# Side work beside a feed-forward stage: stepped by the time of the products, the modulation rows fetched whole through GpSimd's queue

## The chip, the cores and the metric

One core of one Trainium2 chip runs the whole program once. The metric is the device time of that run in microseconds (us), lower being better. The core's engines are TensorE (PE; its weight loads are listed as PEld), VectorE (DVE), ScalarE (ACT), GpSimd (POOL) and SyncE (SP, which here only issues transfers).

## The reference

Two transformer blocks follow each other on 512 tokens of 1024 features, all in fp32. What this case turns on is the first block's feed-forward layer, and two things of the second block that depend on its weights and on `c_2`, not on the tokens:

```python
# end of block 1 (FF1): D_FF = 2816
x = x + (silu(h2 @ w_gate) * (h2 @ w_up)) @ w_down
# block 2: the modulation, six vectors of 1024 = 48 rows of 128
c_act = silu(c)
mod = (c_act @ w_mod + b_mod)
sh1, sc1, g1, sh2, sc2, g2 = split(mod, 6)
h = rms(x, norm1_w) * (1 + sc1) + sh1
...
y_ssm = s5(u, lam_re, lam_im, log_dt, b_re, b_im, ...)   # powers of a complex diagonal, from weights alone
x = x + g1 * (mixed @ w_out)
h2 = rms(x, norm2_w) * (1 + sc2) + sh2
x = x + g2 * conv_ffn(h2, w_up, conv_w, conv_b, w_down)   # FF2
```

The rows 0 to 39 of `mod` hold the five vectors sh1 to sc2; the last eight, 40 to 47, hold g2, which nothing reads before the second feed-forward layer's last additions.

## The kernel before, in words

An fp32 weight block is loaded into a tile `raw` (512 KB, two buffers, issued by SP), split by ACT into `whi` (L365) and by DVE or POOL into the remainder `wlo` (L367); activations are split in the same way into a hi and a lo half (`hl`, `hd`). A product of 128 features by 512 tokens is three matmuls per slice of 128 inputs (hi by hi, lo by hi, hi by lo; all at L259), which sum into one PSUM bank.

FF1 (`ffn`, with `w3` and `w4`) walks over 22 hidden tiles in chunks of 2, 4, 4, 4, 4 and 4. A hidden tile is a gate product and an up product of 24 matmuls each. DVE reads the two banks (`fg`, L1299, and `fu`, L1302), multiplies them (L1303) and makes the lo half of the result `hd` (L494); ACT makes the silu and the hi half. A chunk is followed by the eight down products of the chunk before, each added to a tile of `x` by DVE (L1323). The three `acc` banks are handed round: the fourth product after one may not start until DVE has read that one's bank.

Beside FF1 run two "fillers", generators that `fill()` advances by one step each, once after a hidden tile and once after a down product. `modulation()` makes the 48 rows of `mod`: each row's weights, 128 by 1024, come as two halves of 128x512 (256 KB) through SP's queue into `wm` (three buffers, L1060), and one DVE instruction multiplies a half by silu(c) and sums it (L1061, followed by a short read of the accumulator). `s5_tables()` makes the tables of the S5 scan in four quads: POOL multiplies and adds tiles (`bb`, `bs`, `s5e`, `s5g`; small doubling steps `s5r` and `s5t` at L1077 to L1082, six rounds on 8 to 256 columns), PE transposes `s5e` (L1178) and makes a product of `s5g`; POOL, ACT and SP write the results to DRAM. `LAG` steps lie between parts of one quad.

The engines work in order, each through its own list. Which instruction stands where in a list is decided by a scheduler at build time, from its own estimates; an instruction whose input isn't there holds up all that is behind it on its engine.

FF2 is the second call of `ffn` (`w8`, `w9`); it has seven PSUM banks instead of three and no fillers.

Of the kernel before, what the change touches and what calls it, by code (L numbers as in the profile page):

```python
# [12 lines left out]
ALU = mybir.AluOpType  # L13
# [37 lines left out]
LAG = 4  # L51
# [12 lines left out]
# ------------------------------------------------------------------ layout  # L64
# [29 lines left out]
def w_plan():  # L94
    """name -> list of (input, row0, n_k, columns): one contiguous [128, n_k * n] block each."""
    plan = {}
    plan["w1"] = [("w_in", 0, 8, c) for _, c in W1_CHUNKS]
    plan["w2"] = [("w_out", 0, 8, c) for c in _c256(D)]
    plan["w3"] = [(w, 0, 8, c) for c in _c256(DFF) for w in ("w_gate", "w_up")]
    plan["w4"] = [("w_down", r * P, n, c) for r, n in FCH for c in _c256(D)]  # L100
    plan["w5"] = [("w_in_2", 0, 8, c) for _, c in W5_CHUNKS]
    plan["w6"] = [("w_glu_2", 0, 4, c) for c in _c256(512)]
    plan["w7"] = [("w_out_2", r, 4, c) for r in (0, 512) for c in _c256(D)]
    plan["w8"] = [("w_up_2", 0, 8, c + o) for c in _c256(DFF) for o in (0, DFF)]
    plan["w9"] = [("w_down_2", r * P, n, c) for r, n in FCH for c in _c256(D)]
    return plan
# [18 lines left out]
def pvec(i):  # L125
    """per-partition vectors, name -> [128, n]"""
# [36 lines left out]
def consts():  # L163
    """constants of the shapes alone, name -> [128, n]"""
    f = np.float32
    o = {}
    p = np.arange(P)[:, None]
    o["ident"] = np.eye(P, dtype=f)
    o["onesD"] = np.full((P, P), 1.0 / D, f)
    o["ones512"] = np.full((P, P), 1.0 / 512, f)  # L170
    y = np.arange(512)[None]
    dist = p + 384 - y
    o["dist"] = np.where(dist >= 0, dist, BIG).astype(f)
    mult = ((dist <= 128) * 1 + (dist % 4 == 0) * 1 + (dist % 16 == 0) * 1) * (dist >= 0)
    o["nlm"] = np.where(mult > 0, -np.log(np.maximum(mult, 1)), BIG).astype(f)
    n = np.arange(32)[None, None]
    t = (np.arange(NT)[None, :, None] * P + p[:, :, None])
    dc = t - (16 * n + 31)
    o["distc"] = np.where((dc >= 0) & (n < 31), dc, BIG).astype(f).reshape(P, NT * 32)
    o["rsum"] = (p % 32 == np.arange(32)[None]).astype(f)  # L180
    o["bd"] = ((p // HD) == (np.arange(P)[None] // HD)).astype(f) / HD
    o["sgn"] = np.where(p < 64, -1.0, 1.0).astype(f)
    return o
# [46 lines left out]
# ------------------------------------------------------------------ kernel  # L230
def build(tc, I, out, PV, PVN, CS, CSN, CS1, CSN1):
# [11 lines left out]
    def copy(cat, n, dst, src, scale=None):  # L243
        """on the scalar engine or on the vector engine"""
# [39 lines left out]
    # ---- constants and per-partition vectors  # L284
# [18 lines left out]
    def tables(after=None, name="natural_log_exp_and_others"):  # L303
        """activation tables that the next functions share"""
        if after is None:
            nc.scalar.preload_act_table_set(name)
        else:
            with tc.issue_after(after.ins if hasattr(after, "ins") else after):
                nc.scalar.preload_act_table_set(name)
# [3 lines left out]
    # ---- weights: load, split into two 12-bit parts whose sum is the weight  # L313
# [10 lines left out]
    def cut(name, j):  # L324
        """block j as pieces: (first k, last k, first column, last column) each, with its source"""
# [11 lines left out]
    class _Lazy:  # L337
# [3 lines left out]
        def get(self):  # L341
            """the hi and lo parts; the pieces that come next are on their way too"""
# [29 lines left out]
    def hold_after(piece):  # L372
        """no piece beyond this one is prepared ahead of need"""
        limit[0] = queue.index(piece) + 1

    def go_on(*after):
        """pieces are prepared ahead again, behind the instructions given"""
# [65 lines left out]
    def proj_f(ps, w, x, m, k0=0, cs=ALL):  # L443
        """ps[m-feature, token] = W[:, m].T @ x"""
# [4 lines left out]
    def proj_group(group, x, order, cs=ALL):  # L449
        """several (ps, w, m) at once, the contraction outermost"""  # L450
# [6 lines left out]
    def proj_late(ws, x, early, late, done):  # L457
        """all 8 feature tiles; the first three wait for the late part of x last"""
# [13 lines left out]
    def proj_t(ps, w, x, t, n, o=0):  # L472
        """ps[token, o:o + n] = x[:, token].T @ W"""
# [13 lines left out]
    def split_scaled(dst, src, scale_col):  # L487
        """dst hi/lo of src * scale_col"""
# [7 lines left out]
    def rsqrt_(o, ms, scale=1.0):  # L496
        """o = (ms * scale + eps) ** -0.5, from the tables"""
# [3 lines left out]
    def rsqrt_m2(pool, tag, r, ms):  # L501
        """r = -2 * (ms + eps) ** -0.5, with a Newton step"""
# [6 lines left out]
    def head_norm(pool, wide, dsts, src, nh):  # L509
        """dsts[i][tok, heads, dup, 64] = -128 * src[tok, heads, 64] / rms, the heads in order"""  # L510
# [19 lines left out]
    # gains with the factors that the norms leave open: -1/128 per head norm, -1/2 per feature norm  # L530
# [12 lines left out]
    # ================================================================ block 1  # L543
# [6 lines left out]
    # ---- x, its squares, the unscaled normed input; the first products run along as the tiles of x come in  # L550
# [50 lines left out]
    # ---- bias tables of the causal attentions  # L601
# [11 lines left out]
    # compress chain inputs  # L613
# [11 lines left out]
    # ---- keys, values and gates of the sparse attention; queries and keys of all heads  # L625
# [15 lines left out]
    def kv_p(n):  # L641
        """two query tiles at a time"""
# [28 lines left out]
    def turn2(src):  # L671
        """both query tiles of a pair of heads side by side"""
# [6 lines left out]
    def kv_x(n):  # L679
        """hi and lo of the keys, the same on both halves of the partitions"""  # L680
# [12 lines left out]
    def qa_x(t):  # L693
        """the hi part of the queries on the lower half of the partitions, the lo part on the upper half"""
# [31 lines left out]
    # ---- compressed keys and values  # L726
# [65 lines left out]
    # ---- compressed branch, all tiles at once  # L792
# [28 lines left out]
    # ---- group norm of a finished feature tile, split for the next product  # L821
# [20 lines left out]
    # ---- softmax of one query tile, 4 heads  # L842
# [58 lines left out]
    # ---- stick-breaking: what is left of the stick before a key is the product of 1 - sigmoid over the later keys  # L901
# [32 lines left out]
    # ---- dilated  # L934
# [24 lines left out]
    # ---- short convolution  # L959
# [43 lines left out]
    def tok_norm(pool, parts, r, w="onesD", cs=ALL):  # L1003
        """-2 / rms of every token, on all partitions; the parts add up to the squares"""
# [26 lines left out]
    # ---------------------------------------------------------------- feed-forward 1, with work of block 2 beside it  # L1031
# [18 lines left out]

    def modulation():
# [3 lines left out]
        mh = s5p.tile([P, 2, 48], F32, name="mh")  # L1055
        yield
        for j in range(48):
            for n in range(2):
                wm = s5p.tile([P, 512], F32, tag="wm", bufs=3, name="wm")
                nc.sync.dma_start(wm, I["wmod"][j][:, n * 512:(n + 1) * 512])  # L1060
                V.tensor_tensor_reduce(wm, wm, cb[:, n * 512:(n + 1) * 512], 1.0, 0.0, ALU.mult, ALU.add, mh[:, n, j:j + 1])  # L1061
            yield
        V.tensor_tensor(modT, mh[:, 0], mh[:, 1], op=ALU.add)
        V.tensor_tensor(modT, modT, V1("b_mod"), op=ALU.add)
        dbg("mod", modT)
        yield

    def s5_tables():
# [3 lines left out]
        def cmul(o_r, o_i, a_r, a_i, b_r, b_i, shape, E):  # L1072
            """o = a * b, complex; o may not overlap a or b"""
# [41 lines left out]
        # (a - 1) / lambda  # L1115
# [17 lines left out]
        # mag ** 8 and the rotations of 8, 16, .. 256 steps  # L1133
# [14 lines left out]
        for q in range(4):  # L1148
# [16 lines left out]
            # input to the state at the end of a chunk of 8 tokens  # L1165
# [17 lines left out]
            # state to output, powers 0..8  # L1183
# [11 lines left out]
            # within a chunk  # L1195
# [15 lines left out]
            # rotations of 0..63 chunks  # L1211
# [11 lines left out]
    fillers = [s5_tables(), modulation()]  # L1223

    def fill():
        for f in fillers:
            next(f, None)

    def ffn(wn_up, wn_down, hin, hidden, add_down, after=lambda: None, start=None, tail=None, banks=(acc,)):
# [4 lines left out]
        def up(c):  # L1234
            r, n = FCH[c]
            for j in range(r // 2, (r + n) // 2):
                ws = weights(wn_up, 2 * j), weights(wn_up, 2 * j + 1)
                for m in range(2):
                    ps = []
                    for a in range(2):  # L1240
# [4 lines left out]
                        ps.append(p_)  # L1245
                    hid[2 * j + m] = hidden(2 * j + m, *ps)
                    after()

        def down(c):
            r, n = FCH[c]  # L1250
            last = c == len(FCH) - 1
            for k in range(8 if not (last and tail) else 8 - TAIL):
# [3 lines left out]
                after()  # L1256
# [9 lines left out]
    def norm_tail(pool, tot, r, after, hold, before=None, TAIL=TAIL, NPOS=NPOS):  # L1266
        """the last feature tiles by halves of the tokens: the norm of one half runs beside the products of the other"""
# [42 lines left out]
    def sum_squares(tot, k, src, cs, sq):  # L1310
        """adds to tot, except for the last one, which is returned"""
# [21 lines left out]
    def modulated(n, r, dst, cs, tmp):  # L1333
        """hi/lo of x * r * norm_w * (1 + sc) + sh"""
# [13 lines left out]
    def start_u(cs):  # L1348
        if cs is HALVES[0]:
            for f in fillers:  # L1350
                for _ in f:
# [15 lines left out]
    # ================================================================ block 2  # L1367
# [48 lines left out]
    # ---- S5: chunks of 8 tokens; partitions hold (place, channel) or the state  # L1416
# [21 lines left out]
    def crossed(dst, src, t, sign):  # L1438
        """the imaginary part times t into the real rows, and minus the real part times t into the imaginary rows"""
# [55 lines left out]
    # ---- k, v, q  # L1495
    tokn = {}

    def kv_p(n):
        """two query tiles at a time"""
# [34 lines left out]
    # ---- sliding-window attention  # L1534
# [4 lines left out]
    def keep(k, src, cs, tot, first, gain, n, scale=1.0):  # L1539
        """the hi/lo of a finished feature tile times its gain, and its squares; the norm is applied after the product"""  # L1540
# [13 lines left out]
    def swa_s(n):  # L1554
        """softmax of query tile i, the 4 heads of one key/value head"""
# [57 lines left out]
    # ---- gated linear unit, and its share of the output projection  # L1613
# [71 lines left out]
    # ---------------------------------------------------------------- feed-forward 2  # L1685
# [26 lines left out]
    ffn("w8", "w9", h2, hidden2, down2, start=started, banks=(tr, sc, acc) if B2 else (acc,))  # L1712
# [28 lines left out]
```

## Time and profile before

| what | value |
|---|---|
| runs | 1321.51, 1324.22 and 1327.34 us, median 1324.22 us |
| profiled execution, first to last instruction (span) | 1323.2 us |
| PE busy | 1247.0 us, 94% of the span |
| DVE busy | 864.9 us, 65% |
| ACT, POOL busy | 501.5 us, 38%; 386.4 us, 29% |
| mean granted clock of TensorE | 0.964 of full |

The profile has no other time of its own execution than the span; it lies between the lowest and the median run. Busy shares are means over stages with different limits: FF1 runs from 319 us to some 718 us, the attention part of block 2 follows, FF2 begins at about 970 us. A waiting time counts only where the engine that waits is the one that the rest waits for.

### The profile page before, as it was taken

The page shows a single profiled execution, that of the slowest core. Times are in us where ns is not written, and L with a number is a line of the kernel's source. Part 1 is how long each engine was busy: PE and PEld are TensorE (multiplying, and loading weights), DVE is VectorE, ACT ScalarE, POOL GpSimd, SP SyncE. Part 2 cuts the span into 40 slices and gives each one's busy share as a digit, 9 for nine tenths or more (in the row PEclk, how much of TensorE's full clock was granted, in tenths as well). Part 3 has the DMA queues.
Part 4 walks back from the last instruction along what each step waited for, and adds up shares of the span by engine and source line. Part 5 has one row for each costly group of instructions (what it writes and reads, how often), then busy time and mean ns, then how long its engine had stood idle before and what let it go on. Part 6 is the DMA issues. An engine that isn't in the chain of part 4 may idle for free.

```text
span 1323.2 us, 17207 instructions
## 1 busy us (share of the span) xinstructions
PE 1247.0 (94%) x6269; PEld 1005.0 (76%) x6269; DVE 864.9 (65%) x1615; ACT 501.5 (38%) x862; POOL 386.4 (29%) x403
## 2 busy tenths in 40 slices
PE   7999999999979878999999989979899999999998
PEld 6888765667857657788888978757888888888887
DVE  7668768767988878745445778795855443435362
ACT  5334466445213122322233432663454333333330
POOL 3000004012327439092511143025152423232300
PEclk8999999999999999999999986779899999999999
DMA  5431111126567676643434763331132423232321
GB/s 213 140 123 49 50 32 49 51 77 197 160 198 252 196 248 200 187 147 111 145 109 156 268 175 116 80 96 58 39 99 84 135 85 107 82 108 82 105 87 63
DMA packets 163668, 164.11 MB, mean 124 GB/s; under 512 B 12160, under 2 KB 127760, under 8 KB 163584
## 3 DMA queue, kind: packets, MB, share of 16 engines
q1 hardware_dynamic: 154240, 146.43, 36.2%
q0 software_dynamic: 4256, 12.29, 3.0%
q10 hardware_dynamic: 5088, 4.29, 1.0%
q8 instruction: 49, 0.80, 0.3%
q14 instruction: 35, 0.29, 0.1%
HBM read 149.39 MB, written 15.43 MB: 125 GB/s over the span
## 4 chain that ended last, share of the span: by engine, by line
PE 53%; DVE 16%; DMA 8%; issue 4%; ACT 2%; POOL 0%; DVEq 0%; SPq 0%; ACTq 0%; POOLq 0%
PE acc L259 31%; PE sc L259 10%; PE tr L259 9%; DMA wm<-in_wmod_dram 6%; DVE wm L1061 3%; DMA raw<-in_w_dram 2%; DVE wlo L367 2%; PE po L259 1%; ACT whi L365 1%; DVE hd L494 1%; DVE z L1441 1%; DVE x L1655 1%; DVE z L1442 1%; PE tr L1591 0%; DVE sqsum L1317 0%
## 5 line engine op out<-in xcount | busy, mean ns | idle before, releaser
L259 PE MATMUL acc<-hl,whi 128*128 128x512 f32 (+1 forms) x1624 | 489.5, 385 | 20.9 <-DVE fg L1299 7.5
L259 PEld LDWEIGHTS acc<-hl,whi 128*128 128x128 f32 x1624 | 298.8, 192 | 90.3 <-issue 19.1
L365 ACT ACTIVATE whi<-raw 128x1024 fp32r<-128x1024 f32 (+1 forms) x187 | 193.9, 1039 | 378.4 <-PE acc L259 178.0
L259 PE MATMUL acc<-hl,wlo 128*128 128x512 f32 (+1 forms) x812 | 311.2, 383 | 0.0
L367 DVE TENSOR_TENSOR wlo<-raw,whi 128x1024 fp32r<-128x1024 f32 (+1 forms) x133 | 170.3, 1282 | 67.4 <-ACT whi L365 64.7
L367 POOL TENSOR_TENSOR wlo<-raw,whi 128x1024 fp32r<-128x1024 f32 x54 | 132.2, 2450 | 265.9 <-ACT whi L365 265.9
L259 PEld LDWEIGHTS acc<-hl,wlo 128*128 128x128 f32 x812 | 155.1, 191 | 32.3 <-issue 2.4
L259 PE MATMUL acc<-hd,whi 128*128 128x512 f32 (+1 forms) x472 | 146.4, 393 | 19.3 <-DVE fu L1302 9.2
L259 PEld LDWEIGHTS acc<-hd,whi 128*128 128x128 f32 x472 | 87.9, 191 | 42.7 <-issue 12.7
L259 PE MATMUL acc<-whi,hl 128*128 128x256 f32 (+1 forms) x544 | 111.2, 295 | 1.6 <-ACT tok L246 1.6
L1061 DVE CUSTOM_DVE_ANT_0 wm<-wm,cb 128x512 f32<-128x512 f32 x96 | 87.1, 929 | 30.3 <-DMA wm<-in_wmod_dram 29.3
L259 PEld LDWEIGHTS acc<-whi,hl 128*128 128x128 f32 x544 | 91.1, 199 | 6.2 <-ACT tok L246 3.0
L259 PE MATMUL acc<-hd,wlo 128*128 128x512 f32 (+1 forms) x236 | 92.5, 392 | 0.0
L259 PE MATMUL acc<-wlo,hl 128*128 128x256 f32 (+1 forms) x272 | 79.9, 294 | 0.5 <-DVE wlo L367 0.5
L259 PE MATMUL tr<-hl,whi 128*128 128x512 f32 (+1 forms) x240 | 72.8, 386 | 0.0
L259 PE MATMUL sc<-hl,whi 128*128 128x512 f32 x208 | 64.9, 393 | 0.0
L914 POOL TENSOR_SCALAR_AFFINE_SELECT keep<-keep 128x128 f32<-128x128 f32 x16 | 9.3, 595 | 185.2 <-ACT keep L908 184.4
L259 PEld LDWEIGHTS acc<-wlo,hl 128*128 128x128 f32 x272 | 54.3, 200 | 2.6 <-DVE wlo L367 1.0
L259 PEld LDWEIGHTS acc<-hd,wlo 128*128 128x128 f32 x236 | 45.3, 192 | 9.5
L259 PEld LDWEIGHTS tr<-hl,whi 128*128 128x128 f32 x240 | 44.5, 188 | 9.8
L1323 DVE TENSOR_TENSOR x<-x,acc 128x512 f32<-128x512 f32 (+1 forms) x49 | 31.9, 655 | 28.8 <-PE acc L259 28.7
L259 PE MATMUL tr<-hl,wlo 128*128 128x512 f32 (+1 forms) x120 | 46.3, 386 | 0.0
(422 smaller groups left out, 1963.8 us busy)
## 6 DMA issues: line engine op xcount, KB each, us to landing
raw<-in_w_dram SPq DMA_DIRECT2D x177, 512.0 KB, 4.3
wm<-in_wmod_dram SPq DMA_DIRECT2D x96, 256.0 KB, 3.9
xk<-in_xT_dram SPq DMA_DIRECT2D x16, 256.0 KB, 4.7
d_g<-s5g POOLq DMA_DIRECT2D x4, 576.0 KB, 4.3
gt<-d_g SPq DMA_DIRECT2D x4, 576.0 KB, 4.0
w1c<-in_w1k_dram SPq DMA_DIRECT2D x8, 256.0 KB, 5.7
w1c<-in_w1v_dram SPq DMA_DIRECT2D x8, 256.0 KB, 7.1
raw<-in_w_dram SPq DMA_DIRECT2D x8, 256.0 KB, 2.7
```

Source lines behind the costliest of these rows:

```text
L259: nc.tensor.matmul(o, lhsT=l, rhs=r, start=start, stop=stop, **k)
L365: act(hi[:, :m], raw[:, :m], AF.Copy)
L367: E.tensor_tensor(lo[:, :m], raw[:, :m], hi.bitcast(F32)[:, :m], op=ALU.subtract)
L494: V.tensor_tensor(dst[:, 1], src, dst.bitcast(F32)[:, 0], op=ALU.subtract)
L914: G.affine_select(g[:, d], g[:, d], fill=1.0, **past)
L1061: V.tensor_tensor_reduce(wm, wm, cb[:, n * 512:(n + 1) * 512], 1.0, 0.0, ALU.mult, ALU.add, mh[:, n, j:j + 1])
L1323: V.tensor_tensor(x[k][:, cs], x[k][:, cs], ps[:, cs], op=ALU.add)
L1441: V.scalar_tensor_tensor(dst[re], src[im], sign, t[im], op0=ALU.mult, op1=ALU.mult)
L1442: V.scalar_tensor_tensor(dst[im], src[re], -sign, t[re], op0=ALU.mult, op1=ALU.mult)
L1655: V.tensor_tensor(x[k][:, cs], x[k][:, cs], t[:, cs], op=ALU.add)
```

## The change

`fill` now takes the time of the product beside it: each filler has a rate, and is advanced whenever time times rate has summed up to a whole step. `ffn` calls it with 5.5 after each product of a hidden tile (twice per tile, before it was once) and with 0.7 per slice after a down product. `LAG` goes from 4 to 2. A row of the modulation is fetched whole (128x1024, 512 KB, two buffers) by a transfer that GpSimd issues, and reduced by one DVE instruction. Only rows 0 to 39 belong to FF1; rows 40 to 47 are made in FF2, one step after each product, with a second copy of silu(c).

```diff
-LAG = 4
+LAG = 2
+NWM = 2
+S5_RATE = 0.185
+MOD_RATE = 0.14
...
+    mh = cpool.tile([P, 48], F32, name="mh")
+
+    def mod_rows(pool, cb, j0, j1):
+
+        for j in range(j0, j1):
+            wm = pool.tile([P, D], F32, tag="wm", bufs=NWM, name="wm")
+            nc.gpsimd.dma_start(wm, I["wmod"][j])
+            V.tensor_tensor_reduce(wm, wm, cb, 1.0, 0.0, ALU.mult, ALU.add, mh[:, j:j + 1])
+            yield
+        V.tensor_tensor(modT[:, j0:j1], mh[:, j0:j1], V1("b_mod")[:, j0:j1], op=ALU.add)
+        yield
+
     def modulation():
         cb = s5p.tile([P, D], F32, name="cb")
         nc.sync.dma_start(cb, I["cbc"])
         act(cb, cb, AF.Silu)
-        mh = s5p.tile([P, 2, 48], F32, name="mh")
         yield
-        for j in range(48):
-            for n in range(2):
-                wm = s5p.tile([P, 512], F32, tag="wm", bufs=3, name="wm")
-                nc.sync.dma_start(wm, I["wmod"][j][:, n * 512:(n + 1) * 512])
-                V.tensor_tensor_reduce(wm, wm, cb[:, n * 512:(n + 1) * 512], 1.0, 0.0, ALU.mult, ALU.add, mh[:, n, j:j + 1])
-            yield
-        V.tensor_tensor(modT, mh[:, 0], mh[:, 1], op=ALU.add)
-        V.tensor_tensor(modT, modT, V1("b_mod"), op=ALU.add)
...
+        yield from mod_rows(s5p, cb, 0, 40)
...
-    fillers = [s5_tables(), modulation()]
-
-    def fill():
+    fillers = [[s5_tables(), S5_RATE, 0.0], [modulation(), MOD_RATE, 0.0]]
+
+    def fill(us):
+
         for f in fillers:
-            next(f, None)
...
+            f[2] += us * f[1]
+            while f[2] >= 1.0:
+                f[2] -= 1.0
+                next(f[0], None)
...
+                        if a == 0:
+                            after(5.5)
                     hid[2 * j + m] = hidden(2 * j + m, *ps)
-                    after()
+                    after(5.5)
...
-                after()
+                after(0.7 * n)
...
-    ffn("w8", "w9", h2, hidden2, down2, start=started, banks=(tr, sc, acc) if B2 else (acc,))
+    cb2 = fp.tile([P, D], F32, name="cb2")
+    nc.gpsimd.dma_start(cb2, I["cbc"])
+    act(cb2, cb2, AF.Silu)
+    late = mod_rows(fp, cb2, 40, 48)
+    ffn("w8", "w9", h2, hidden2, down2, after=lambda us: next(late, None), start=started, banks=(tr, sc, acc) if B2 else (acc,))
```

Comments were removed too, so that lines of the new kernel carry other numbers: L1082 to L1087 are the former L1077 to L1082, L370 the former L367, L497 the former L494, L1310, L1313 and L1314 the former L1299, L1302 and L1303.

The first place is POOL's list in FF1, first quad. In the rows below `wm` is a row of the modulation weights, `s5t` and `s5r` are the doubling steps, `bb`, `bs` and `s5u` parts of the second quad's input. Before, POOL's list has no rows and these steps stand alone; after, the rows 8 to 14 stand between them (8 to 11 in the first line, 12 and 13 on either side of one step, 14 at the end):

```order
L1060 DMA wm<-in_wmod_dram 128x1024 x4
L1083 TENSOR_TENSOR s5t<-s5r,ro_i 128x8
...
L1083 TENSOR_TENSOR s5t<-s5r,ro_i 128x64
L1060 DMA wm<-in_wmod_dram 128x1024
L1084 TENSOR_TENSOR s5r<-s5r,s5t 128x8x8
L1060 DMA wm<-in_wmod_dram 128x1024
L1086 TENSOR_TENSOR s5t<-s5r,ro_r 128x64
...
L1175 TENSOR_TENSOR s5e<-bb,pw_r 128x1024
L1087 TENSOR_TENSOR s5r<-s5r,s5t 128x8x32
L1060 DMA wm<-in_wmod_dram 128x1024
```

Between row 11 and row 12 stand 19 small steps, between row 13 and row 14 another 19 instructions, among them `s5e` on 1024 columns. A row can be fetched only after them.

The second place is DVE's list at the same rows. The reductions of rows 10 to 14 stand between the readings of the banks (`fg`, `fu`), the products' second halves (`wlo`) and `hd`:

```order
L1061 ISA wm,mh<-wm,cb 128x1024
L497 TENSOR_TENSOR hd<-fu,hd 128x512
L1061 ISA wm,mh<-wm,cb 128x1024
L1310 SCALAR_TENSOR_TENSOR fg<-acc,r_3100 128x512
L370 TENSOR_TENSOR wlo<-raw,whi 128x512
L1061 ISA wm,mh<-wm,cb 128x1024
L1061 ISA wm,mh<-wm,cb 128x1024
L1313 SCALAR_TENSOR_TENSOR fu<-acc,r_3100 128x512
L370 TENSOR_TENSOR wlo<-raw,whi 128x512
L1314 TENSOR_TENSOR fu<-fu,fg 128x512
L1061 ISA wm,mh<-wm,cb 128x1024
L497 TENSOR_TENSOR hd<-fu,hd 128x512
```

(the short reads of the accumulator are left out.) Behind each reduction stands the reading of a bank that PE will want again. The last of the 40 reductions stands behind the gate bank of the 13th hidden tile, at the same place as the last of the 96 did before.

The third place is POOL's list at the start of FF2. Before it is `wlo` alone, 44 of them; after, the copy of c and the rows 40 to 47 stand among the first eleven:

```order
L370 TENSOR_TENSOR wlo<-raw,whi 128x1024 x3
L1724 DMA cb_8607<-in_cbc_dram 128x1024
L370 TENSOR_TENSOR wlo<-raw,whi 128x1024
L1060 DMA wm<-in_wmod_dram 128x1024 x2
L370 TENSOR_TENSOR wlo<-raw,whi 128x1024
L1060 DMA wm<-in_wmod_dram 128x1024
L370 TENSOR_TENSOR wlo<-raw,whi 128x1024 x2
L1060 DMA wm<-in_wmod_dram 128x1024 x2
```

SP's list loses all its `wm` transfers, which before stood two to four at a time between the loads of `raw`.

## Rows read from the trace of the kernel before

**Rows 1.** Two stretches of FF1, then FF2: busy time of each engine, clock, transfers.
```profile
319.00:545.50 226.50, 199.77 (x848) 157.05 (x847) 191.11 (x403) 58.98 (x80) 107.87 (x134) 0.95 0.68 212
545.50:718.00 172.50, 171.51 (x775) 137.93 (x774) 90.72 (x104) 52.22 (x67) 64.67 (x113) 1.00 0.42 129
980.00:1320.00 340.00, 339.19 (x1467) 275.15 (x1465) 153.74 (x194) 113.79 (x142) 89.42 (x37) 1.00 0.32 94
```

**Rows 2.** The products' line alone (L259) in two stretches: PE, PEld, clock, transfers.
```profile
319.00:545.50 226.50, 197.19 (x832) 154.30 (x831) 0.95 0.68 212
340.00:360.00 20.00, 20.00 (x88) 16.24 (x87) 1.00 0.72 217
```

**Rows 3.** Waits from 319 to 545.5 us: in total, times, the longest.
```profile
DVE wm L1061 <- DMA wm<-in_wmod_dram: 29.3, 25, 3.0
PE acc L259 <- DVE fg L1299: 11.0, 4, 4.0
PE acc L259 <- DVE fu L1302: 9.7, 3, 6.9
```

**Rows 4.** DVE's groups of instructions, 319 to 545.5 us: busy, mean ns, idle before.
```profile
L1061 DVE CUSTOM_DVE_ANT_0 wm<-wm,cb 128x512 f32<-128x512 f32 x96 | 87.1, 929 | 30.3 <-DMA wm<-in_wmod_dram 29.3 <-ACT cb L1054 1.0
L367 DVE TENSOR_TENSOR wlo<-raw,whi 128x1024 fp32r<-128x1024 f32 (+1 forms) x33 | 41.4, 1255 | 2.7 <-ACT whi L365 2.7
L494 DVE TENSOR_TENSOR hd<-fu,hd 128x512 fp32r<-128x512 f32 x12 | 14.8, 1236 | 0.0
L1299 DVE SCALAR_TENSOR_TENSOR fg<-acc,r 128x512 f32<-128x512 f32 x13 | 8.9, 681 | 0.0
L1061 DVE DVE_READ_ACCUMULATOR2_ANT mh<- 128x1 f32 x96 | 7.6, 79 | 0.0
```

**Rows 5.** Timeline of DVE: start, duration, idle time before and what ended it.
```profile
391.82 2.14 DVE L1061 CUSTOM_DVE_ANT_0 wm<-wm,cb 128x512 f32<-128x512 f32 x1 [0.50 <-DMA wm<-in_wmod_dram]
...
397.51 0.68 DVE L1061 CUSTOM_DVE_ANT_0 wm<-wm,cb 128x512 f32<-128x512 f32 x1
...
969.55 4.17 DVE L1694 SCALAR_TENSOR_TENSOR cf<-acc,pv,cf 128x511 f32<-128x511 f32 x6 [6.48 <-ACT cf L1692]
```

**Rows 6.** Transfers issued from 319 to 545.5 us: count, KB each, median us to landing.
```profile
wm<-in_wmod_dram SPq DMA_DIRECT2D x96, 256.0 KB, 3.9
raw<-in_w_dram SPq DMA_DIRECT2D x29, 512.0 KB, 4.8
d_rot<-s5r POOLq DMA_DIRECT2D x2, 512.0 KB, 4.8
```

**Rows 7.** Timeline of POOL, first quad, while DVE is busy.
```profile
390.88 2.53 POOL L1189 TENSOR_TENSOR s5g<-s5bc,pw_r 128x1152 f32<-128x1152 f32 x1 [20.68 <-PE tr L1178]
...
396.72 0.58 POOL L1192 DMA_DIRECT2D d_g<-s5g  x1 [0.30 <-POOL s5g L1191]
...
405.28 0.21 POOL L1078 TENSOR_TENSOR s5t<-s5r,ro_i 128x8 f32<-128x8 f32 x1 [6.41 <-DMA d_et<-s5et]
...
409.11 0.67 POOL L1082 TENSOR_TENSOR s5r<-s5r,s5t 128x8 f32<-128x8 f32 x1
...
415.28 1.16 POOL L1078 TENSOR_TENSOR s5t<-s5r,ro_i 128x64 f32<-128x64 f32 x1
...
424.13 0.61 POOL L1078 TENSOR_TENSOR s5t<-s5r,ro_i 128x256 f32<-128x256 f32 x1
...
433.11 2.05 POOL L1170 TENSOR_TENSOR s5e<-bb,pw_r 128x1024 f32<-128x1024 f32 x1
```

**Rows 8.** Timeline of POOL, third quad, with no more rows on DVE.
```profile
568.30 0.20 POOL L1078 TENSOR_TENSOR s5t<-s5r,ro_i 128x8 f32<-128x8 f32 x1
...
574.11 0.30 POOL L1078 TENSOR_TENSOR s5t<-s5r,ro_i 128x64 f32<-128x64 f32 x1
...
580.18 0.61 POOL L1078 TENSOR_TENSOR s5t<-s5r,ro_i 128x256 f32<-128x256 f32 x1
...
589.44 0.45 POOL L1163 TENSOR_TENSOR bs<-bs,s5u 128x128 f32<-128x128 f32 x1
```

More of the change, by code (lines that the diff above doesn't have):

```diff
@@ L1054, in modulation @@
         act(cb, cb, AF.Silu)
-        mh = s5p.tile([P, 2, 48], F32, name="mh")
         yield
-        for j in range(48):
-            for n in range(2):
-                wm = s5p.tile([P, 512], F32, tag="wm", bufs=3, name="wm")
-                nc.sync.dma_start(wm, I["wmod"][j][:, n * 512:(n + 1) * 512])
-                V.tensor_tensor_reduce(wm, wm, cb[:, n * 512:(n + 1) * 512], 1.0, 0.0, ALU.mult, ALU.add, mh[:, n, j:j + 1])
-            yield
-        V.tensor_tensor(modT, mh[:, 0], mh[:, 1], op=ALU.add)
-        V.tensor_tensor(modT, modT, V1("b_mod"), op=ALU.add)
-        dbg("mod", modT)
-        yield
+        yield from mod_rows(s5p, cb, 0, 40)
     def s5_tables():
@@ L1221, in s5_tables, with ffn @@
             yield
-    fillers = [s5_tables(), modulation()]
-    def fill():
+    fillers = [[s5_tables(), S5_RATE, 0.0], [modulation(), MOD_RATE, 0.0]]
+    def fill(us):
         for f in fillers:
-            next(f, None)
-    def ffn(wn_up, wn_down, hin, hidden, add_down, after=lambda: None, start=None, tail=None, banks=(acc,)):
+            f[2] += us * f[1]
+            while f[2] >= 1.0:
+                f[2] -= 1.0
+                next(f[0], None)
+    def ffn(wn_up, wn_down, hin, hidden, add_down, after=lambda us: None, start=None, tail=None, banks=(acc,)):
         banks = itertools.cycle(banks)
@@ L1350, in start_u @@
             for f in fillers:
-                for _ in f:
+                for _ in f[0]:
                     pass
```

## The prediction

> **What bounds the kernel now.** I read the stretches first. FF1 falls into two: from 319 to 545.5 us PE is busy 199.8 of 226.5 us at a granted clock of 0.95, and after that, as in FF2, it is busy almost all the time at full clock [rows 1]. So PE is the limit everywhere around this change except in the first stretch, and only there can anything be won. At the full pace of 20.00 us for 88 matmuls, 0.2273 us each, the 832 matmuls of the products would take 189.1 us instead of 197.2 [rows 2]. The stretch thus loses 26.7 us to an idle PE and some 8 us to the clock, 35 us in all: the ceiling of any gain here.
>
> Next, why PE idles. It waits for DVE to read banks, `fg` and `fu`, never for anything nearer to the change [rows 3]. DVE in turn is busy 191.1 us of the stretch [rows 1], and of its idle 35.4 us (226.5 - 191.1) 29.3 are spent before a reduction whose weights haven't landed [rows 3]; no wait of DVE for a bank shows among its groups [rows 4]. That is the reading the rest hangs on: in this stretch DVE is the chain. Its work and its waits add up to the stretch, PE follows through three banks, and the last reduction ends it (PE is full from there). The order of the changed kernel puts its last reduction behind the same bank as before, that of the 13th hidden tile. So the new stretch is the sum of DVE's work and DVE's waits up to there.
>
> DVE's work is not all its own. `fg`, which reads PSUM and one SBUF tile, takes 681 ns; a half row's reduction, two SBUF tiles, has a mean of 929 ns, and single ones run from 0.68 to over 2 us [rows 4, 5]. The 2.14 us one at 391.82 lies under POOL's `s5g` of 390.88 to 393.41 [rows 5, 7]. `hd`, 1236 ns on tiles of the same size, is stretched too [rows 4].
>
> The Trainium skill, "SBUF — State Buffer", section "Who interferes with whom", states such a rule: a VectorE instruction with two SBUF inputs and a GpSimd instruction that reads SBUF exclude each other for a whole instruction, one with a single SBUF input isn't touched. The trace agrees, `fg` with 681 ns against `hd` with 1236 ns [rows 4].
>
> **The change, part by part, as DVE's sum.**
>
> Work taken off DVE: 96 half rows become 40 whole ones, the work of 80 halves. 87.1 us x 16/96 = 14.5 us go [rows 4]; with them 56 of 96 reads of the accumulator, 56 x 79 ns = 4.4 us [rows 4]. 191.1 - 18.9 = 172 us.
>
> Contention: POOL now has three quads' work and a part of the fourth beside the rows, where two and a part of the third lay before (107.9 us of POOL in the stretch, 64.7 us in the next [rows 1]). What the stretching costs now is (929 - 680) ns x 96 for the reductions and (1236 - 681) ns x 12 for `hd`, 24 + 7 = 31 us [rows 4, 5]. The change adds between nothing (while DVE waits, nothing is stretched, and it has fewer reductions) and half as much again, 15 us. I take 5, nearer to nothing for these two reasons.
>
> Waits at gaps: this is the dear part. A row's transfer is issued by POOL in its turn. With two buffers POOL may be two rows ahead, but whatever S5 work stands between two rows keeps the second back. A gap of G us on POOL makes DVE wait G + 0.6 (an issue by POOL, like that of `d_g`, 0.58 us [rows 7]) less what DVE has to do meanwhile: a whole row, some 1.24 us (an estimate: two undisturbed halves, 0.68 us each [rows 5], less the overlap of their ends), and what stands between the two reductions, each 0.68. POOL's times come from the same entries in two quads: the first, with DVE busy [rows 7], and the third, with no rows on DVE [rows 8].
> - First place, rows 12 and 14. The 19 steps from `s5t` on 8 columns to `s5t` on 64: from 405.28 to 416.44, less some 1.9 us for a wait and other entries, 9.3 us [rows 7]; from 568.30 to 574.41, 5.7 us [rows 8]. Between the reductions `fg` and `wlo`: 9.3 + 0.6 - 2.6 = 7, or 4. The second 19, with `s5e`: 416.44 to 435.16 less 1, 17.7 us [rows 7]; 574.41 to 589.89 less 2.1, 13.4 us [rows 8]. Between the reductions `fu`, `wlo` and the product: less 3.3, which gives 15, or 11. Together 22, or 15.
> - Second place, rows 20 and 22. Row 20 stands behind `s5g` and its sum, 390.88 to 396.42, 5.5 us [rows 7], an issue and eight small entries: some 8 us, less 4 of DVE's own: 4. Row 22 stands behind 27 steps up to `s5t` on 256 columns: 409.11 to 424.74, 15.6 us [rows 7], or 11.0 (568.30 to 580.79 less 1.5 for seven entries ahead) [rows 8]; less 2: 14, or 9. Together 18, or 13.
> - Third place, rows 33 to 38. Row 36 stands behind 20 of these 27 steps, 11.6 or 8.2 us by count, less 0.6: 11, or 7.5. Row 33 stands behind `s5g` (0 to 2), 37 and 38 a product apart (0 to 4). Together 17, or 8.
>
> The sum is 57 us on contended times, 36 on quiet ones. Since DVE stands idle in the later part of each gap, neither holds throughout; I take the middle, 46.
>
> The rhythm between gaps: nine rows stand beside the eight down products of the second chunk, where a cycle of two buffers allows one row in (4.8 + 0.6 + 1.24)/2 = 3.3 us (a 512 KB transfer takes 4.8 us, from SP's queue or from POOL's [rows 6]), 30 us for what PE does in 22 (8 x 12 x 0.2273). With DVE's other work there it is 0 to 8; I take 5. The idle time that isn't a wait for rows stays, 35.4 - 29.3 = 6.
>
> What costs nothing: SP loses 96 issues, so `raw` no longer stands behind halves that wait for buffers. But DVE waits for `whi` only 2.7 us in the stretch [rows 4], which bounds that gain; I count none. The rows move as many bytes each as before, 21 instead of 25 MB, at a transfer share of 0.68 [rows 1]. `LAG` and the rates move the transposes and tables forward; PE doesn't wait for POOL.
>
> The page "DMA: Bandwidth & Descriptors" of the Trainium skill, section "Anatomy of one DMA — SWDGE (gpsimd) path", gives by its formula some 3.2 us for 512 KB; an estimate by that would make the rhythm free, and the sum 5 us less. The traced 4.8 us is used.
>
> FF2: eight rows, 10 us of DVE, in a stage where DVE is busy 153.7 of 340 us [rows 1]. Its first reduction stands ahead of the first `cf`, which began at 969.55 after an idle 6.48 [rows 5]. The copy of c must be fetched, made silu of and be followed by a row: I estimate two transfers, 2 x 4.8 us, from 963 us, so DVE begins some 3 us late, beside seven banks that give PE 7 x 5.5 us to run on. Taken as 0; with the cover gone, +10.
>
> **Sum.** 172 + 5 + 46 + 5 + 6 = 234 us against 226.5: +7.5. 1323.2 + 7.5 is 1331; the median of the runs lies 1 us above the profiled span, so 1332 us. At the ends: 172 + 0 + 36 + 0 + 6 = 214 (-12.5, 1312) and 172 + 15 + 57 + 8 + 6 = 258 (+31.5, 1356). It balances at gap waits of 38.5 us.
>
> **The rivals.**
>
> *The other side: DVE comes late to its rows.* If at each of the seven gaps the row ahead has been lying in its buffer for some 3 us (one row and a `wlo` of 1.26 us still before DVE [rows 4]), the quiet 36 becomes 15. Then DVE needs 172 + 15 + 11 = 198, still above PE's own 189, and the kernel takes 1324 + 198 - 226.5 = 1296; with half of that lead, waits of 25, it is 1306, which I give it. From waits under 38.5 us on, the change gains. For it speaks that DVE is busy 191 of 226.5 us before [rows 1]; against it that DVE waited 25 times for rows before, with three buffers and a queue that did little else [rows 3].
>
> *No change:* the gaps run at quiet times and contention stays: 172 + 5 + 38 + 5 + 6 = 226, 1324 us. What eight rows give, the gaps take.
>
> *FF2's start not covered:* 1332 + 10 = 1342.
>
> *Rows that land late from GpSimd.* If POOL's part in starting a transfer is held up by DVE, each row lands a few us later: 40 rows by 1 us in the rhythm of two buffers give up to +20 us, 1352. Against it: `d_rot`, 512 KB from POOL's queue, landed in the same 4.8 us as `raw` from SP's [rows 6]. The Trainium skill speaks for it, "SBUF — State Buffer", section "SBUF: two separate sides": transfers that GpSimd issues are starved while VectorE copies in a two-port mode, and it advises another queue.
>
> **How the numbers follow.** About 0.5%, 6.6 us, is what a measurement of this kernel can tell from no change. Chances: the main case 0.48 (its own range 1315 to 1352; slower 0.32, within the bound 0.14, faster 0.02), DVE late 0.22 (faster 0.20, same 0.02), no change 0.18 (same 0.14, slower 0.02, faster 0.02), FF2 0.05 and late rows 0.07 (slower). Together faster 0.24, same 0.30, slower 0.46. The range goes from 1305 to 1350; above lie the worst gaps and most of the late rows, below an unhindered lead, 2 in 10 together.
>
> **What would show it.** In the changed profile, DVE's wait for `wm` should grow from 29.3 to about 50 us with single waits of 7 to 15 us, before rows 12, 14, 22 and 36, each behind a run of `s5r` and `s5t` on POOL; DVE's reductions should be 40 in FF1 and sum to under 75 us; PE's waits for `fg` and `fu` should lie right behind those waits, the stretch to the last of the 40 should take about 234 us, and PE should be full after it and in FF2. I am wrong if DVE's wait stays under 38 us, if rows land in 6 us or more, or if the stretch ends elsewhere than at the last reduction.

## The result and the profile after

The changed kernel takes 1341.58 us (median of 4 runs, 1340.69 to 1344.02) against 1322.87 us before (the three runs of the table of before and a fourth): a ratio of 1.0137, 95% interval 1.0114 to 1.0160. It is slower by 18.7 us; 8 were forecast. The profiled executions have spans of 1339.3 and 1323.2 us, 16.1 us apart.

Where the 16.1 us lie is read from four marks. FF1's last sum of squares ahead of it ends 1.6 us later than before; the last of the 40 reductions and the sum with `b_mod` end the first stretch at 561.0 instead of 545.5 us, so the stretch takes 240.4 instead of 226.5, 13.9 us more; from there to the end everything stays 15 to 18 us late. The stretches of the changed kernel, columns as in [rows 1]:

```profile
320.60:561.00 240.40, 199.07 (x862) 155.86 (x861) 188.99 (x290) 61.66 (x86) 160.09 (x234) 0.94 0.61 190
561.00:734.50 173.50, 172.53 (x761) 139.74 (x760) 87.77 (x103) 49.78 (x61) 28.27 (x53) 1.00 0.38 116
984.00:1336.00 352.00, 351.12 (x1522) 284.77 (x1520) 173.79 (x221) 121.34 (x153) 100.59 (x46) 1.00 0.36 108
```

PE is full from 561 us on and in FF2, as it was. In the first stretch DVE is still the chain: 188.99 us busy, and the rest, 51.4 us, idle. Before it was 191.1 and 35.4 [rows 1]. Eight rows less have bought only 2 us of busy time, and 16 us of idle time have come on top. POOL's busy time there went from 107.9 to 160.1 us; 22 of the 52 us more are issues of rows (a line below). TensorE's clock isn't in the difference: the mean granted clock of the stretch is 0.94, before 0.95, and PE takes 199.07 us for 862 matmuls, before 199.77 for 848.

DVE's groups and the waits of the stretch (line numbers of the changed kernel), to be held against [rows 3, 4]:

```profile
L1061 DVE CUSTOM_DVE_ANT_0 wm<-wm,cb 128x1024 f32<-128x1024 f32 x40 | 63.1, 1586 | 38.4 <-DMA wm<-in_wmod_dram 38.4
L370 DVE TENSOR_TENSOR wlo<-raw,whi 128x1024 fp32r<-128x1024 f32 (+1 forms) x33 | 54.8, 1661 | 7.3 <-ACT whi L368 7.2
L1083 DVE TENSOR_TENSOR s5t<-ro_i 128x32 f32<-128x32 f32 x8 | 6.1, 766 | 0.0
L1084 DVE TENSOR_TENSOR ro_r<-ro_r,s5t 128x32 f32<-128x32 f32 x8 | 5.8, 723 | 0.0
```
```profile
DVE wm L1061 <- DMA wm<-in_wmod_dram: 38.4, 18, 7.7
DVE wlo L370 <- ACT whi L368: 7.2, 5, 2.9
DVE s5bc L1191 <- DMA s5bc<-in_s5bc_dram: 2.9, 3, 2.1
```
```profile
PE acc L262 <- DVE fu L1313: 15.3, 2, 8.5
PE acc L262 <- DVE x L1334: 11.1, 5, 4.7
PE acc L262 <- DVE fg L1310: 8.8, 5, 2.8
```

The reductions sank from 87.1 to 63.1 us, but 33 `wlo` rose from 41.4 to 54.8, and DVE's own small S5 steps rose too. The two groups shown were, in the kernel before:

```profile
L1078 DVE TENSOR_TENSOR s5t<-ro_i 128x32 f32<-128x32 f32 x8 | 1.7, 216 | 0.0
L1079 DVE TENSOR_TENSOR ro_r<-ro_r,s5t 128x32 f32<-128x32 f32 x8 | 3.3, 412 | 0.0
```

All six groups of these steps went from 13.6 to 22.3 us. The wait for rows rose from 29.3 to 38.4 us, in 18 pieces instead of 25. The rows themselves land as fast as `raw` does:

```profile
wm<-in_wmod_dram POOLq DMA_DIRECT2D x39, 512.0 KB, 4.7
raw<-in_w_dram SPq DMA_DIRECT2D x29, 512.0 KB, 4.8
```

One new group stands on POOL: it now waits itself, before it may issue a row.

```profile
L1060 POOL DMA_DIRECT2D wm<-in_wmod_dram x39 | 22.1, 566 | 57.3 <-DVE mh L1061 41.2 <-DVE ro_i L1087 4.4 <-DVE ro_i L1085 3.8
```

The first place of the prediction, in the timelines of DVE, POOL and PE:

```profile
387.45 1.31 DVE L1061 CUSTOM_DVE_ANT_0 wm<-wm,cb 128x1024 f32<-128x1024 f32 x1 [2.20 <-DMA wm<-in_wmod_dram]
...
394.09 7.92 DVE L1061 CUSTOM_DVE_ANT_0 wm<-wm,cb 128x1024 f32<-128x1024 f32 x1 [4.12 <-DMA wm<-in_wmod_dram]
401.94 0.08 DVE L1061 DVE_READ_ACCUMULATOR2_ANT mh<- 128x1 f32 x1
401.94 1.21 DVE L1061 CUSTOM_DVE_ANT_0 wm<-wm,cb 128x1024 f32<-128x1024 f32 x1
...
403.08 0.68 DVE L1313 SCALAR_TENSOR_TENSOR fu<-acc,r 128x512 f32<-128x512 f32 x1
...
406.31 1.22 DVE L1061 CUSTOM_DVE_ANT_0 wm<-wm,cb 128x1024 f32<-128x1024 f32 x1 [1.34 <-DMA wm<-in_wmod_dram]
```
```profile
381.42 0.52 POOL L1083 TENSOR_TENSOR s5t<-s5r,ro_i 128x8 f32<-128x8 f32 x1
...
389.43 0.60 POOL L1060 DMA_DIRECT2D wm<-in_wmod_dram  x1 [0.19 <-DVE fg L1310]
...
390.91 0.31 POOL L1086 TENSOR_TENSOR s5t<-s5r,ro_r 128x64 f32<-128x64 f32 x1
...
394.09 0.61 POOL L1082 TENSOR_TENSOR s5r<-s5r,ro_r 128x256 f32<-128x256 f32 x1
...
395.65 0.60 POOL L1083 TENSOR_TENSOR s5t<-s5r,ro_i 128x256 f32<-128x256 f32 x1
...
398.25 2.00 POOL L1175 TENSOR_TENSOR s5e<-bb,pw_r 128x1024 f32<-128x1024 f32 x1
400.21 0.71 POOL L1087 TENSOR_TENSOR s5r<-s5r,s5t 128x256 f32<-128x256 f32 x1
402.31 0.60 POOL L1060 DMA_DIRECT2D wm<-in_wmod_dram  x1 [1.39 <-DVE mh L1061]
```
```profile
403.91 1.19 PE L262 MATMUL acc<-hd,whi 128*128 128x512 f32 x2 [8.54 <-DVE fu L1313]
```

Row 12 is issued at 389.43, behind the 19 steps that began at 381.42, and DVE waits 4.12 us for it. Its reduction then takes 7.92 us instead of 1.22. The next run of S5 steps stands on POOL from 390.91 to 400.92 without a pause, and the reduction ends 1.1 us after that run, about as long as it takes undisturbed; so the run held it up. Behind it stands the read of the `fu` bank, and PE has waited 8.54 us for that. POOL in turn can't issue row 14 at 400.92 but waits until 402.31, for that same reduction. So at this place a gap costs twice: once while the row isn't there, once while the row is and POOL keeps DVE from it.

FF2 went as reckoned: before the first reduction, DVE was idle for 7.86 us; it began at 986.60 us, `cf` at 987.75, 18.2 us later than before where the rest is 16 late, and PE is busy 351 of 352 us.

### The profile page after: what moved, and what is told of

It reads as the page before. It is cut to its first block, busy times and chain, and to the rows that moved or that the text cites. A ratio compares the mean times of both kernels' runs of the same rounds, so it can differ in the third digit from the quotient of the medians.

```text
span 1339.3 us, 16964 instructions
## 1 busy us (share of the span) xinstructions
PE 1244.8 (93%) x6269; PEld 1002.7 (75%) x6269; DVE 872.8 (65%) x1519; ACT 501.8 (37%) x863; POOL 409.0 (31%) x452
## 4 chain that ended last, share of the span: by engine, by line
PE 51%; DVE 13%; DMA 6%; POOL 6%; issue 6%; ACT 2%; SPq 0%; DVEq 0%; POOLq 0%; ACTq 0%
PE acc L262 30%; PE sc L262 10%; PE tr L262 9%; DMA raw<-in_w_dram 3%; DMA wm<-in_wmod_dram 3%; DVE wlo L370 2%; PE po L262 1%; ACT whi L368 1%; DVE wm L1061 1%; POOL s5t L1086 1%; DVE x L1666 1%; DVE z L1464 1%; POOL s5g L1196 1%; DMA s5bc<-in_s5bc_dram 1%; PE tr L1602 0%
## 5 line engine op out<-in xcount | busy, mean ns | idle before, releaser
L370 DVE TENSOR_TENSOR wlo<-raw,whi 128x1024 fp32r<-128x1024 f32 (+1 forms) x133 | 178.1, 1341 | 65.5 <-ACT whi L368 62.7
L370 POOL TENSOR_TENSOR wlo<-raw,whi 128x1024 fp32r<-128x1024 f32 x54 | 133.8, 2478 | 240.6 <-ACT whi L368 240.5
L1061 DVE CUSTOM_DVE_ANT_0 wm<-wm,cb 128x1024 f32<-128x1024 f32 x48 | 73.9, 1546 | 55.3 <-DMA wm<-in_wmod_dram 55.2
L1337 POOL DMA_DIRECT2D d_x<-x x12 | 6.5, 542 | 146.9 <-DVE x L1334 146.9
```

Source lines behind the costliest of these rows:

```text
L370: E.tensor_tensor(lo[:, :m], raw[:, :m], hi.bitcast(F32)[:, :m], op=ALU.subtract)
L1061: V.tensor_tensor_reduce(wm, wm, cb, 1.0, 0.0, ALU.mult, ALU.add, mh[:, j:j + 1])
L1337: nc.gpsimd.dma_start(d_x[k][:, cs], x[k][:, cs])
```

## The experiments

Two theories. One: the rows' issues stand behind S5 work on POOL, and DVE waits for them. Two: S5 work, packed more densely into the stretch, stretches DVE's instructions. The prediction used both, with waits of 46 + 5 us for the first, where the kernel before had 29, and 5 us for the second. A third came up with the profile after: POOL and DVE hold each other up through the two buffers.

Each ratio below is to the kernel before in runs on the same chip. "FF1" is the time in the profile from the last sum of squares ahead of it to the last read of a gate bank: 361.1 us before (317.9 to 679.0), 376.0 after (319.5 to 695.5). An edit changes more than its own lines: the scheduler orders the engines' lists anew for each kernel. In the kernel before and in the changed one the last row that FF1 makes is reduced behind the 13th gate bank, in rows_sp and nwm3 behind the 10th. So each run tells what an edit is worth with the order that came with it.

**rows_sp** and **s5_slow** each undo one part of the change: the first diff is that of rows_sp, the second that of s5_slow.

```diff
-            nc.gpsimd.dma_start(wm, I["wmod"][j])
+            nc.sync.dma_start(wm, I["wmod"][j])
```
```diff
-LAG = 2
+LAG = 4
-        for f in fillers:
+        if not half:
+            next(fillers[0][0], None)
+        for f in fillers[1:]:
...
-                            after(5.5)
+                            after(5.5, True)
```

> The changed kernel with its row transfers issued by SP instead of GpSimd; all else as changed. Theory one (the S5 work that stands between two issues on POOL makes DVE wait): DVE's wait for wm in FF1 falls from 38.4 us to 15 to 25 us, the last of the 40 rows ends two hidden tiles earlier, and the time is 1318 to 1328 us. Theory two (the loss comes from S5 work packed into the same stretch, whose GpSimd instructions stretch DVE's): DVE stays busy as long, wlo stays at a mean of 1.6 us, and the time is 1333 us or more.

Measured: 1324.14 us, ratio 1.0017 (0.9994 to 1.0040); FF1 363.9 us. DVE's wait for rows fell as the first theory has it:

```profile
DVE wm L1061 <- DMA wm<-in_wmod_dram: 15.3, 15, 2.0
```

`wlo` kept a mean of 1.58 us, as the second has it. The 40th row is through at 505 instead of 560 us, much more than the two hidden tiles expected, yet FF1 gains 12 us. So the queue is worth 12 us of FF1, and 16 us by the ratios (1.0137 and 1.0017); `wlo` is stretched as before.

> The changed kernel with the S5 filler at its old pace (one step after each hidden tile and each down product, LAG 4); rows whole, from GpSimd, at the new pace. Theory one (S5 work ahead of the issues): fewer gaps, wait for wm 25 to 35 us. Theory two (stretching by packed S5 work): wlo's mean in FF1 falls from 1.66 us to about 1.25 us and the time to 1322 to 1330 us. If only GpSimd's queue as such is dear, the time stays at 1336 to 1342 us.

Measured: 1322.65 us, ratio 1.0011 (0.9990 to 1.0031); FF1 359.4 us. POOL was busy 119.8 of 240 us instead of 159.7; the mean of a reduction fell from 1.59 to 1.35 us, the wait for rows from 38.4 to 31.9. `wlo`'s mean fell to 1.54 us only, not to 1.25, so that half of what the second theory said was a miss; why `wlo` stays long there isn't shown. The old pace of S5 alone brings the kernel back to where it was.

**pace_only**, the kernel before with the new pace and nothing else (rates 0.185 and 0.14, `LAG` 2, the two calls per hidden tile, on 96 half rows from SP's queue).

> The kernel before with the new pace alone (rates, LAG 2, two calls per hidden tile); 96 half rows on SP's queue as before. Theory two (stretching by packed S5 work): DVE's work grows by 12 to 17 us and the time is 1333 to 1340 us. Theory one (GpSimd's issues): no gaps behind S5 work, the time is 1320 to 1328 us.

Measured: 1333.62 us, ratio 1.0080 (1.0050 to 1.0109); FF1 376.0 us, as long as with the whole change. The stretch to the last reduction:

```profile
318.50:563.00 244.50, 205.93 (x882) 161.46 (x880) 206.06 (x402) 61.65 (x86) 155.13 (x201) 0.93 0.65 208
```
```profile
DVE wm L1063 <- DMA wm<-in_wmod_dram: 31.0, 23, 5.0
```

DVE has practically the instructions of before, 402 instead of 403, and is busy 206.1 instead of 191.1 us; its wait for rows is the old one, 31.0 against 29.3. This is the second theory with the rows on SP's queue: 47 us more of POOL beside the rows go with 15 us more of DVE and 15 us more of FF1. Of DVE's 15 us the row reductions have 4 (90.7 instead of 87.1), `wlo` 4 (45.5 instead of 41.4), and DVE's own S5 steps 6 (20.0 instead of 13.6).

**queue_only**, the kernel before with its 96 half rows issued by GpSimd.

```diff
-                nc.sync.dma_start(wm, I["wmod"][j][:, n * 512:(n + 1) * 512])
+                nc.gpsimd.dma_start(wm, I["wmod"][j][:, n * 512:(n + 1) * 512])
```

> The kernel before with its 96 half rows issued by GpSimd instead of SP, all else as before (old pace, 48 rows in FF1, three buffers). Theory one (S5 work between the issues on POOL makes DVE wait): DVE's wait for wm in FF1 rises from 29.3 to 40 us or more, single waits over 5 us, and the time is 1328 to 1340 us. If the pace alone carries the loss, the wait stays near 30 us and the time at 1318 to 1326 us.

Measured: 1345.80 us, ratio 1.0185 (1.0145 to 1.0226); FF1 385.4 us.

```profile
DVE wm L1061 <- DMA wm<-in_wmod_dram: 56.8, 30, 10.3
```
```profile
POOL wm L1060 <- DVE mh L1061: 92.2, 45, 7.9
```

The wait is as the first theory has it; the time lies 6 us above its range. In FF1 the queue alone is dearer than the whole change, 385.4 against 376.0 us (by the ratios, 1.0185 and 1.0137, the intervals touch): DVE waits 56.8 us for rows, nearly twice as long as before, and POOL 92.2 us for DVE. It has 96 issues on POOL there where the change has 40, and all 48 rows in FF1.

**tail_only**, the kernel before with rows 40 to 47 in FF2, and **no_tail**, the changed kernel with all rows in FF1 (`mod_rows(s5p, cb, 0, 48)`, and nothing late).

> The kernel before with rows 40 to 47 made in FF2 (halves, SP's queue, two rows after each product), all else as before. If DVE is the chain of the first stretch of FF1, 16 half rows less are worth their 14.5 us and a part of their waits: 1306 to 1313 us. If PE or the transfers set the stretch, 1318 to 1324 us. In FF2 nothing is lost by either.

Measured: 1317.39 us, ratio 0.9974 (0.9954 to 0.9995); FF1 349.7 us in the profile, 11.4 less than before. FF1 agrees with the first case; the ratio over ten runs is a gain of 3 us, less than the 7 to 14 expected. The profiled execution, with a span of 1309.5 us, is the fastest of the ten (1311.41). The direction is shown, the size isn't.

> The changed kernel with all 48 rows in FF1, none in FF2. If DVE is the chain of the stretch, eight rows more cost their reduction of 1.6 us and a wait of 1 us each, some 20 us: 1352 to 1364 us. If they hide beside other work, 1338 to 1345 us, and the change lost nothing less than its full 19 us to the rest.

Measured: 1360.70 us, ratio 1.0313 (1.0275 to 1.0351); FF1 396.5 us. Eight rows more in FF1 lengthen it by 20.5 us, as the first case has it: DVE is the chain there, and the late rows are the part of the change that pays, some 20 us of it.

**rot_memset** and **no_rot** leave out the rotations: in the changed kernel the six doubling rounds become 16 memsets of 512 columns per quad, or 2 (`range(2)`, one for each half of the tile).

```diff
-            for n in range(6):
-                w_ = 1 << n
-                ...
+            for n in range(16):
+                G.memset(rt[:, n % 2], 1.0)
```

> The changed kernel, in which the six doubling rounds of each quad's rotation (36 instructions that read and write SBUF) are replaced by 16 memsets of 512 columns, which only write; this leaves the rotations out. POOL still stands between the rows for a similar time. Theory two (GpSimd instructions that read SBUF stretch DVE's): the mean of a row's reduction falls from 1.59 us to under 1.35, wlo's from 1.66 us to under 1.4, and the time to 1318 to 1328 us, with DVE's wait for rows still at 30 us or more. Theory one (the waits alone): DVE's waits and the time stay within 6 us of 1340.

Measured: 1317.17 us, ratio 0.9973 (0.9950 to 0.9995); FF1 353.2 us, in a profile of the fastest of the ten runs.

```profile
L1221 POOL MEMSET s5r<- 128x512 f32 x64 | 30.4, 531 | 0.0
```
```profile
L1061 DVE CUSTOM_DVE_ANT_0 wm<-wm,cb 128x1024 f32<-128x1024 f32 x39 | 55.8, 1438 | 23.2 <-DMA wm<-in_wmod_dram 23.1
L370 DVE TENSOR_TENSOR wlo<-raw,whi 128x1024 fp32r<-128x1024 f32 (+1 forms) x38 | 52.9, 1392 | 9.4 <-ACT whi L368 9.3
```

POOL is nearly as busy as in the changed kernel, 153 against 160 us, yet some 22 us of the time are gone (by the ratios). That speaks for the second theory: 30 us of POOL's work only write, and its computing on SBUF data, by the sums of its groups, is some 80 us where the changed kernel has 126. The means came near what it expected, 1.44 us (under 1.35) and 1.39 (under 1.4). But the wait for rows fell too, to 23 us where 30 were expected, and the scheduler put the last row one hidden tile later. A quad's memsets take 7.6 us of POOL, its rotation steps took 16.5 (49.4 us for three quads in the changed kernel), so that the runs of work between rows became shorter as well. This run doesn't part the two theories. The Trainium skill, "SBUF — State Buffer", section "Who interferes with whom", makes this difference: a VectorE instruction with two SBUF inputs contends with GpSimd instructions that read SBUF, not with those that only write. The means here agree in direction: 1.59 to 1.44 us for a reduction, 1.66 to 1.39 for `wlo`.

> The changed kernel without the six doubling rounds (two memsets per quad in their place; the rotations are left out). Both the gaps and the stretching shrink: the wait for rows falls to 15 to 25 us, and the time to 1305 to 1318 us by both theories. If it stays over 1330 us, the rotation steps on POOL are not where the loss is, and the row transfers themselves or the transposes are.

Measured: 1321.91 us, ratio 1.0013 (0.9997 to 1.0030); FF1 358.3 us; wait for rows 22.6 us, as expected, the time 4 us above it. With fewer instructions on POOL it is no faster than with the memsets; `wlo` stayed at 1.67 us there. Why isn't settled. The two runs together show that the rotations cost 16 to 22 us where they are (by the ratios), not how these split.

**nwm3**, the changed kernel with `NWM = 3`.

> The changed kernel with three buffers for rows instead of two. If POOL and DVE hold each other up through the two buffers (POOL stood 41 us of FF1 before an issue because DVE hadn't reduced the row two back), POOL's wait falls under 25 us, DVE's wait for wm under 28, and the time is 1322 to 1332 us. If the S5 work ahead of an issue and the stretching are what costs, a third buffer changes neither: 1334 to 1342 us.

Measured: 1325.65 us, ratio 1.0061 (1.0039 to 1.0083); FF1 369.3 us.

```profile
DVE wm L1061 <- DMA wm<-in_wmod_dram: 20.3, 5, 6.4
```
```profile
POOL wm L1060 <- DVE mh L1061: 21.5, 11, 8.0
```
```profile
PE tr L1183 <- POOL s5e L1177: 14.0, 2, 13.2
```

Both waits halve, from 38.4 and 41.2 us, and by the ratios 10 us of the time are gone, 7 of them in FF1. That is what the third theory expected: with two buffers an issue waits for the reduction two rows back, the S5 work behind the issue waits too, and the next row comes later for it. It isn't shown by this alone, since a row more in store would shorten DVE's wait behind a run of S5 work by the first theory too. And POOL's wait for DVE is no price in itself:

```profile
POOL wm L1060 <- DVE mh L1061: 65.2, 23, 7.5
POOL wm L1060 <- DVE mh L1061: 82.4, 19, 11.3
```

The first line is of s5_slow, the second of no_rot; both are faster than the changed kernel, and POOL waits for DVE longer. What comes out next in nwm3 is PE's wait for `s5e` of POOL, 14.0 us, where no other profile has more than 2.1 (no_rot): there POOL is the late one.

**sp_slow**, **sp_s5_125** and **sp_slow3** look for a better kernel: rows from SP's queue, rows 40 to 47 in FF2, and S5 at its old pace (sp_slow), at a rate of 0.125 with `LAG` 2 (sp_s5_125), or at its old pace with `NWM = 3` (sp_slow3).

> The changed kernel with its rows issued by SP and S5 at its old pace: whole rows, two buffers, rows 40 to 47 in FF2 remain. If the two parts that cost add up (each came to 12 to 17 us of FF1 when it was undone alone), the time is 1303 to 1312 us. If undoing one part leaves nothing for the other, because DVE then keeps up with PE anyhow, it is 1314 to 1322 us.

Measured: 1312.07 us, ratio 0.9927 (0.9902 to 0.9951), at the border between the two cases; FF1 348.0 us. Undoing both parts brings 28 us of FF1, as 12 and 17 added up. What is left of the change beside tail_only (FF1 349.7 us, ratio 0.9974) is that rows come whole, in two buffers and at the new pace: that costs nothing here.

> The changed kernel with its rows issued by SP and S5 stepped at 0.125 instead of 0.185, LAG 2, so that S5 lies more behind the rows. If the loss is S5 work stretching DVE where DVE is the chain, less of it stands beside the rows: POOL busy under 115 us of 240, time 1303 to 1312 us. If only the queue of the rows counts, it is like the rows on SP alone, 1318 to 1328 us; if S5 ends too late for block 2, 1320 us or more with a wait in the attention stage.

Measured: 1312.71 us, ratio 0.9951 (0.9931 to 0.9970); FF1 353.8 us; POOL busy 120.8 of 240 us. Time and POOL's share both come out just above the second theory's bounds (1312 us and 115), and it is no better than S5 at its old pace with sp_slow.

> Rows issued by SP, S5 at its old pace, rows 40 to 47 in FF2, and now three buffers for whole rows. With two buffers DVE waited 10.6 us for rows in FF1. If DVE is still the chain there, a third buffer takes most of that away: 1302 to 1309 us. If PE is already the chain (DVE waited 30 us for banks there), nothing is left to gain: 1308 to 1316 us.

Measured: 1303.07 us, ratio 0.9895 (0.9862 to 0.9927); FF1 345.5 us. The third buffer takes the wait for rows down to 3.9 us. This kernel beats both: the kernel before by about 14 us, the changed one by some 32 (by the two ratios). Its stretch to the last reduction:

```profile
318.80:467.20 148.40, 133.32 (x559) 105.83 (x558) 137.79 (x259) 43.51 (x59) 69.12 (x74) 0.94 0.74 242
```

The 40 rows are through after 148 instead of 240 us, and POOL has only 69 us of S5 beside them.

## Why the prediction was right in direction and short in size

The reading it hung on held: DVE is the chain of the first stretch, its work and waits add up to it (189.0 + 51.4 = 240.4), the stretch ends with the last reduction, and PE is full behind it and in FF2. no_tail shows the same from the other side.

Term by term, in us:

| term | predicted | measured in the changed kernel |
|---|---|---|
| DVE's work without new contention | 172 | 177 = 191.1 - 14.5 (not seen apart) |
| contention | 5 (0 to 15) | 12 = 189.0 - 177 |
| waits for rows: gaps and rhythm | 46 + 5 (36 to 65) | 38.4 |
| other idle time of DVE | 6 | 13.0 = 51.4 - 38.4 |
| stretch | 234 | 240.4 |

The 5 us between 172 and 177 are a misreading: 4.4 us were taken off for reads of the accumulator, but such a read costs DVE no time. It lies inside the end of its reduction, and the next instruction starts with it (the one at 401.94).

The contention was sized too low, and put on the wrong instructions. I priced it on the reductions and on `hd`, and took 5 "nearer to nothing", because DVE would have fewer reductions and would stand idle in the gaps. For these two the reasons held: the reductions took 14 us more than 40 undisturbed ones of 1.22 us, where I had counted 24 before, and `hd` fell from 14.8 to 10.6 us. What the sum left as it was is where the loss lies: 33 `wlo` took 13.4 us more, DVE's own S5 steps 8.7 more. pace_only, which has neither gaps nor fewer reductions, costs 15. Nor does DVE always escape the S5 work by waiting: row 12 landed in the middle of the next run of it (the 7.92 us reduction).

That the direction came out right is in part luck. The wait for rows, the dear part of the forecast, grew by 9 us and not by 22, and its 38.4 us are 0.4 above the bound under which I had called myself wrong. With that wait and the other terms as forecast, the stretch is 172 + 5 + 38.4 + 6 = 221 us, a gain of 5; the change loses because DVE's work came out 12 us higher and its other idle time 7.

The gap waits came out below the middle, near the quiet values: 4.12 us before row 12 (7 or 4 predicted), 7.66 before row 22 (14 or 9), 6.66 before row 36 (11 or 7.5). Only row 14 was far off, 1.34 instead of 15 or 11, since row 12's reduction had eaten that time. At row 12 DVE, and not POOL, was the one held up, which fits POOL's quiet pace. Gap and contention were priced as separate terms, and there they are one: what the one loses, the other gains.

Not in the sum at all was the way back, POOL waiting for DVE before an issue (41.2 us). "POOL may be two rows ahead" was taken as an allowance; it holds S5 back as well. A third buffer gives some 10 us (nwm3); how much of that is the way back isn't shown.

The 7 us that DVE's other idle time grew by are waits for `whi` (7.2 instead of 2.7) and for `s5bc` (2.9, none before). Another 1.6 us lie ahead of FF1. The runs' medians are 18.7 apart where the two profiled spans are 16.1; the difference is within the runs' spread.

The rivals: "DVE comes late to its rows" is out as a whole, since DVE waited 38.4 us for them, more than before, and not 25 or less; row 14 is a place where it was late. "No change" is out: the kernel takes 18.7 us longer. Rows that land late from GpSimd are out as well: 4.7 us against 4.8 for `raw`. FF2's start was covered.

Open is the attention stage between FF1 and FF2: from the first modulated tile of the one normalisation to the last of the other it took 231.6 us before, and between 226 and 233 us in the experiments, so that FF1 times and whole times differ by as much. Nothing here was run on that.

## What to carry to other kernels

A transfer that is issued by an engine with work of its own takes a place in that engine's order: what stands ahead delays the transfer, and the wait for a free buffer delays what stands behind. Where two engines feed each other so, count both directions; a wait of the issuing engine costs only where something that is needed stands behind it. Here an idle queue gave 16 us and a buffer more 10. And side work that makes the bounding engine's instructions longer belongs where that engine has room, not evenly over the time of the products; price it on all that engine's instructions in the stretch, not only on those that the change touches.

## What the runs showed of the hardware

A DVE instruction on two SBUF tiles can be held up not by one GpSimd instruction but by a whole run of them: the 1.22 us reduction took 7.92 us while ten GpSimd instructions followed each other without a pause, and these ran at their undisturbed pace (`s5t` on 256 columns 0.60 us, with no rows on DVE 0.61 [rows 8]). In the whole kernel that is seen once, and once more in no_tail (8.07 us); the longest before was 3.08 us. With 16 memsets a quad in place of 36 instructions that also read SBUF, GpSimd was nearly as busy over the stretch and the kernel some 22 us faster, though each quad's share of the work was shorter too.
